# Three seven-product pairs in the second up stage of a residual block, in place of two

## The chip, the cores and the metric

The kernel runs on one core of one Trainium2 chip. The metric is the device time of one execution in microseconds (us), the median of three runs. TensorE (PE in the profile) multiplies matrices; VectorE (DVE), ScalarE (ACT) and GpSimd (POOL) do the element-wise work; SyncE (SP) issues most of the DMAs and POOL some.

## What is computed

One layer of a residual network on 512 tokens of width 1024 in float32. Only its last part, the channel mixer, is touched by the change:

```
h = rms_norm(x, norm_ffn_g)
up = causal_dwconv(h @ w_up, conv_ffn_w)        # 1024 -> 2 x 2816, three taps
a, b = split(up)
x = x + (silu(a) * b) @ w_down                  # 2816 -> 1024
return rms_norm(x, norm_f_g)
```

`causal_dwconv` weighs each token's value with those of the two tokens before it, column by column.

## The kernel before

**Products.** Everything is held transposed, with the model's columns on the 128 partitions and the 512 tokens along the free axis. A float32 weight is split into a high and a low part (`wh` by ScalarE, L275; `wl` by VectorE, L279), and so are the inputs. A product is the sum of three passes, high by high, low by high and high by low, each a matmul of a 128x128 weight block with 256 tokens.

**Pairs and phases.** The hidden width is 22 blocks of 128. Block `j` of `a` and block `j` of `b` make the up pair `j`. The pairs 0 to 11 are phase 0 and 12 to 21 phase 1 (`PHASES`); after each phase's up stage comes its down stage, in which the finished hidden blocks are multiplied by `w_down`.

**Plain and seven-product pairs.** A plain pair (`block`, `mm3`, L309) is two weight chunks of eight 128x128 blocks (`up2j`, `up2j+1`), each 48 matmuls. A pair listed in `SUP` is done by `seven` instead, a Winograd scheme: of each two-by-two arrangement of weight blocks with the two halves of the tokens, seven products are formed in place of eight (`PROD`, `passes`, L327). Such a pair is two doubles; each double is a chunk `P` of six weight blocks (18 matmuls) and a chunk `F` of eight blocks of weight sums (24 matmuls). The down stages use the same scheme throughout (`STEPS`: 12 doubles in phase 0, 8 in phase 1). A plain pair leaves two PSUM banks, which are multiplied by the norm factor (`mul`, L1171) and run through the three taps (`tap`: one ScalarE and two VectorE instructions, L566, L567, L570). A seven-product pair leaves four banks, which `merge` first adds up (L1192 to L1206) and scales (L1214). `glu` then takes silu of `a` (L1231) and multiplies by `b` on POOL (`ge` for an even pair, L1236; `go` for an odd one, L1243); after an odd pair it forms sums for the down stage (`t13`, `t24`, L1253 to L1258) and splits them (`hl`, L1262 and L1263). For the very last pair, `glu` also calls a Sqrt activation (L1233) for the sake of its table.

**Inputs of the seven-product up pairs.** They need sums of the inputs too (`up_forms`). Phase 0 makes them and stores them in DRAM (`ys`); for phase 1 four tiles `y` are loaded back through one buffer, one after the other (L1084), and split (`parts_of`, L1076 and L1079). That work comes due at the end of the down stage of phase 0 and in the first two weight chunks of phase 1.

**Weight sums.** The `F` chunks are made in DRAM while the kernel runs (`make_forms`): for each group of two doubles six DMAs, `put f0` (512 KB, SP, L208), `add f0` (512 KB, POOL, accumulating, L211), `put f1`, `add f1`, `put f2`, `add f2` (256 KB each), each waiting for the one before it. `GROUPS` says at which call of `slot()` each of the six is issued, and how far the next group is shifted. `slot()` is called twice in every up pair and once in every double of a down stage. In phase 0 the count runs from 8 to 31 in the up stage and from 32 to 43 in the down stage.

**Weights and buffers.** The chunks come in a fixed order (`stream`), loaded by SP up to seven ahead into four buffers for plain and `P` chunks and four for `F` chunks. `split` makes `wh` and `wl` of one chunk, while PE works on the chunk before it; there are two buffers for `wh` and two for `wl`, so a split can start only when PE has finished the chunk two before.

**The order of the small work.** VectorE and ScalarE have more to do between the splits than fits at once, so tasks wait in a list `later`, each with a planned cost and a due chunk. After each split `run_later` releases tasks up to a budget. While a task of an up pair's evacuation (tag `e`) waits, the budget is 4.2 us after a plain chunk, 1.6 after a `P` and 1.2 after an `F` (L290); without one it is 1.7, 1.6 and 0.75. The planned costs are 6.87 us for the merge and the taps of a seven-product pair, 4.2 for the evacuation of a plain pair, and 4.5 for the sums and splits of each two pairs. If no `e` task waits, an evacuation is issued at once. `after_split` makes released tasks follow the latest split on their engine. The framework may otherwise issue an instruction of ScalarE or VectorE ahead of one that was written earlier; matmuls, POOL's products of pairs before the last and DMAs keep the written order.

**The end of an up stage.** At the second chunk of the last pair (L1162 on) the first `P` chunk of the down stage is split. Then, if `e` tasks still wait, they are all issued (`flush_only`) and the first `F` chunk is split (`split()`). If none waits, neither is done there; that `F` chunk is split later, by `seven`, behind the last evacuation and `glu`.

**Banks.** The seven-product pairs of phase 1 use PSUM banks 2 to 5, the plain pairs banks 6, 7, 0, 1 in turn (`turns`).

Of the kernel before, what the change touches and what calls it, by code (L numbers as in the profile page):

```python
# [16 lines left out]
KB = D // P  # L17
# [25 lines left out]
PHASES = ((0, 12), (12, NP))  # L43
# [14 lines left out]
PLAIN = [(m, k) for m in (6, 7) for k in range(*PHASES[1])]  # L58
PCUTS = (0, 8, 12, 20)

SUP = ((1, 2, 5), (14, 16))
XF = (26, 0)
UPD = tuple(tuple(((j, q), (j, q + 1)) for j in js for q in (0, 2)) for js in SUP)
DOUBLES = GATES + UPD[0] + STEPS[0] + UPD[1] + STEPS[1]
NU = [len(GATES), len(GATES + UPD[0] + STEPS[0])]
ND = [NU[i] + len(UPD[i]) for i in range(2)]
GROUPS = {"gate": (2, 4, 1), "up0": (2, 4, 1), "up1": (2, 4, 1), 0: (2, (0, 3, 14, 18, 22, 26), 1), 1: (2, 3, 1)}


@with_exitstack  # L70
def block_kernel(ctx, tc, xT, vecs, wv, win, wmix, wo, wup, wst, wdp, outT):
# [10 lines left out]
    def keep(ins):  # L82
        return tc.keep_in_program_order(ins)
# [45 lines left out]
    def step_chunks(n):  # L129
        m = len(DOUBLES[n])  # L130
        return [(f"P{n}", wst[n, :, : 3 * m * P], 3 * m * P), (f"F{n}", n, 4 * m * P)]
# [10 lines left out]
    for ph, (j0, j1) in enumerate(PHASES):  # L142
        for j in range(j0, j1):
            if j in SUP[ph]:
                stream += step_chunks(n) + step_chunks(n + 1)
# [13 lines left out]
    def after_split():  # L159

        st = ExitStack()
        for ins in order.values():
            st.enter_context(tc.issue_after(ins))
        return st
# [25 lines left out]
    def make_forms(n0, n1, key, start=0):  # L190

        size, step, shift = GROUPS[key]
        if not start:
            make_forms.slot = 0
        cuts = [n0]
        for n in range(n0 + 1, n1 + 1):
            if n == n1 or n - cuts[-1] == size or len(DOUBLES[n]) != len(DOUBLES[cuts[-1]]):
                cuts.append(n)
        for g, (a, b) in enumerate(zip(cuts, cuts[1:])):
            m = len(DOUBLES[a]) * P  # L200
            f = dr.tile([P, b - a, 4 * m], F32, tag=f"f{a}", name=f"f{a}")
            w = wst[a:b].rearrange("n p c -> p n c")
            x0, x1, x2 = w[:, :, 3 * m : 5 * m], w[:, :, 5 * m : 7 * m], w[:, :, 7 * m : 8 * m]
            for n in range(a, b):
                made[n] = f[:, n - a, :]

            def put(dst, src):
                return lambda: keep(nc.sync.dma_start(dst, src))  # L208

            def add(dst, src):  # L210
                return lambda: keep(nc.gpsimd.dma_start(dst, src, accum_op=ALU.add))  # L211

            f0, f1, f2 = f[:, :, : 2 * m], f[:, :, 2 * m : 3 * m], f[:, :, 3 * m :]
            ops = (put(f0, x0), add(f0, x1), put(f1, f[:, :, :m]), add(f1, x1[:, :, m:]), put(f2, f1), add(f2, x2))
            todo_bg.extend((start + (step * k if isinstance(step, int) else step[k]) + shift * g, op) for k, op in enumerate(ops))
        todo_bg.sort(key=lambda w: w[0])
# [30 lines left out]
    def flush_only(tags):  # L247

        while n := [n for n, w in enumerate(later) if set(w[2]) & set(tags)]:
            with after_split():  # L250
                later.pop(n[0])[3]()
# [495 lines left out]
    acc, bank_s, bank_t = ring(2, 0, 1), ring(3, 4), ring(5, 6)  # L747
# [116 lines left out]
    acc = ring(3, 4, 5, 6, 2, 7)  # L864
# [94 lines left out]
    for j in range(KB):  # L959
# [13 lines left out]
        else:  # L973
            if j == GJ:
                acc = ring(3, 4, 2, 7)
# [31 lines left out]
    acc = ring(0, 1, 5, 6, 3, 4, 2, 7)  # L1007
# [89 lines left out]

    po = None
    make_forms(ND[0], ND[0] + len(STEPS[0]), 0)
    make_forms(NU[1], ND[1], "up1", 20)  # L1100
    for j in range(KB):
        slot()
        if j == 0:
# [20 lines left out]
    def turns(*ids):  # L1124
        st = list(ids)

        def f(name):
            f.last = st.pop(0)
            flush((f.last,))
            return bank(f.last, name)  # L1130

        return f

    acc = turns(0, 1, *(2, 3, 4, 5) * 2, 6, 7, 0, 1, 2, 3, 4, 5)
    USETS = dict.fromkeys(SUP[1], (2, 3, 4, 5)) | {1: (2, 3, 4, 5), 2: (6, 7, 0, 1), 5: (6, 7, 0, 1)}
    ssq3 = xp.tile([P, S], F32, tag="ssq", name="ssq3")
# [4 lines left out]
    def up(j, ph, rb2, pu=None):  # L1141
        uu = []

        def tap(i, z):
            u = fp.tile([P, S], F32, tag="fu", name=f"fu{j}{i}", bufs=3)
            taps(u, z, CF + 3 * (2 * j + i))
            uu.append(u)

        if j in SUP[ph]:
            c = 2 * SUP[ph].index(j)  # L1150
            slot()
            seven(
                UPD[ph][c : c + 2], NU[ph] + c, {j: USETS[j]}, lambda q, g: up_form(ph, q, g), of="x",
                done=lambda i, banks, ids: merge(ph, j, banks, ids, rb2, tap, uu),
            )
            slot()
            return
        evacs = []
        for i in range(2):
            slot()  # L1160
            p = pu[i] if pu else block(f"up{2 * j + i}", x1h, x1l, True)
            if i and j + 1 == PHASES[ph][1]:  # L1162
                split_next()
                if any(("e",) in w[2] for w in later):
                    flush_only((("e",),))
                    split()
            z = [None]

            def mul(i=i, p=p, z=z):
                z[0] = fp.tile([P, S], F32, tag="fz", name=f"fz{j}{i}", bufs=4)  # L1170
                nc.vector.tensor_mul(z[0], p, rb2)  # L1171

            evac = [(0.7, mul), (1.4, lambda i=i, z=z: tap(i, z[0]))]
            if i:
                evac.append((0, lambda: glu(ph, j, uu)))
            if any(("e",) in w[2] for w in later):
                later.extend((0, us, (("e",), acc.last) if x == 0 else (("e",),), f) for x, (us, f) in enumerate(evac))
            else:
                for _, f in evac:
                    f()  # L1180
# [141 lines left out]
    X, Y = (6, 7, 0, 1), (2, 3, 4, 5)  # L1322
    for ph, (j0, j1) in enumerate(PHASES):
        if ph:
            acc = turns(*(6, 7, 0, 1) * 4)
            make_forms(ND[1], len(DOUBLES), ph)
        for j in range(j0, j1):
            pu = None
            if j == 0:
                nrm = {}  # L1330

                def mid():
                    nrm["c"] = rstd_col([ssq2], NT, 6, "n2")

                def late():
                    nrm["b"] = rstd_sb(rstd_bc(nrm["c"], NT, 7, "n2"), "n2")

                pu = lead(["up0", "up1"], x1h, x1l, mid, late)
            up(j, ph, nrm["b"], pu)
        if not ph:  # L1340
            up_forms(0, 1)
        flush_only((("e",),))
        seven(
            STEPS[ph], ND[ph], ({0: X, 1: Y, 3: X, 2: Y}, {0: X, 1: Y, 2: Y})[ph],
            lambda q, g: (gh[:, place(ph, q) + g, :], gl[:, place(ph, q) + g, :]),
            done=lambda i, banks, ids: combine(ph, i, banks, ids), tick=True,
        )
        assert not todo_bg
# [188 lines left out]
```

## Time and profile before

| what | us |
|---|---|
| median of three runs | 695.37 (695.27 to 695.41) |
| the profiled execution | 694.18 |
| its span, first to last instruction | 692.4 |
| up stage of phase 1 on PE, first matmul to the first of the down stage | 523.83 to 631.08 |
| PE busy over the span | 683.1 (99%) |
| VectorE busy over the span | 554.2 (80%) |
| ScalarE busy over the span | 368.3 (53%) |

A row of the timeline has the start and the duration in us, the engine, the line of the kernel, the operation, the output and inputs by the program's names, the shapes, the number of instructions merged into the row and, in brackets, how long the engine had been idle before it and what ended that. `dn` is the PSUM output of `seven`, `p_up` that of a plain pair. A matmul's row lasts longer than the step from one matmul to the next, since they are pipelined; so PE's pace is read from the starts. A row of the windows has, for one stretch, its length and the busy time of each engine with the number of instructions, then the granted TensorE clock (1.00 is full), the mean busy share of the 16 DMA engines and GB/s.

### The profile page before, as it was taken

What the parts mean: (1) busy time and instruction counts of PE and PEld (TensorE: products, weight loads), DVE (VectorE), ACT (ScalarE), POOL (GpSimd) and SP (SyncE); (2) the same over time, 40 slices, a digit from 0 to 9 for tenths busy, and PEclk for the clock granted to TensorE, in tenths of its full rate; (3) what the DMA queues carried; (4) which work ended last, traced back from release to release, by engine and by line L of the source; (5) the groups of instructions that cost most, each with busy time, mean ns of one, the idle gap of its engine ahead of it and who ended that gap; (6) DMA issues with size and microseconds to landing.
All of it is one profiled execution on the core that took longest, in us unless ns stands there. A gap on an engine that the chain in (4) does not pass through costs nothing. (4 is left out here: it accounts for less than half of the span.)

```text
span 692.4 us, 14690 instructions
## 1 busy us (share of the span) xinstructions
PE 683.1 (99%) x5936; PEld 680.6 (98%) x5936; DVE 554.2 (80%) x858; ACT 368.3 (53%) x579; POOL 190.5 (28%) x201
## 2 busy tenths in 40 slices
PE   9999999999999999999999999999999999999996
PEld 9999999999999999999999999999999999999995
DVE  6677787877578778769879699998787899988894
ACT  5675755554554444546554555545444544545572
POOL 6134947542020201214400144340100325231000
PEclk9999999999999999999999999999999999999998
DMA  8629999552568586788998498888945996676413
GB/s 308 225 67 293 216 243 204 134 120 92 185 144 221 166 268 205 230 308 213 158 313 241 126 233 222 200 242 231 252 149 167 337 231 157 188 168 182 154 31 122
DMA packets 65012, 137.53 MB, mean 199 GB/s; under 512 B 5760, under 2 KB 30352, under 8 KB 64688
## 3 DMA queue, kind: packets, MB, share of 16 engines
q1 hardware_dynamic: 44664, 107.28, 47.2%
q0 software_dynamic: 18464, 26.03, 23.4%
q10 hardware_dynamic: 1816, 3.29, 1.3%
q8 instruction: 46, 0.75, 0.4%
q14 instruction: 22, 0.18, 0.1%
HBM read 132.31 MB, written 47.71 MB: 260 GB/s over the span
## 5 line engine op out<-in xcount | busy, mean ns | idle before, releaser
L211 POOL DMA_DIRECT2D f<-in_wst_dram x66 | 77.7, 1371 | 27.1 <-DMA f<-f 26.8
L309 PE MATMUL p_up<-x1h,wh_up 128*128 128x256 f32 x416 | 81.2, 276 | 0.0
L309 PE MATMUL p_up<-x1l,wh_up 128*128 128x256 f32 x416 | 81.0, 276 | 0.0
L309 PE MATMUL p_up<-x1h,wl_up 128*128 128x256 f32 x416 | 81.0, 276 | 0.0
L279 DVE TENSOR_TENSOR wl_F<-raw_F,wh_F 128x1024 fp32r<-128x1024 f32 (+1 forms) x42 | 55.9, 1330 | 20.0 <-ACT wh_F L275 20.0
L275 ACT ACTIVATE wh_F<-raw_F 128x1024 fp32r<-128x1024 f32 (+1 forms) x42 | 44.3, 1054 | 39.5 <-PE dn L327 28.7
L309 PEld LDWEIGHTS p_up<-x1h,wh_up 128*128 128x128 f32 x416 | 62.7, 188 | 0.0
L309 PEld LDWEIGHTS p_up<-x1l,wh_up 128*128 128x128 f32 x416 | 62.7, 188 | 0.0
L309 PEld LDWEIGHTS p_up<-x1h,wl_up 128*128 128x128 f32 x416 | 62.6, 188 | 0.0
L309 PE MATMUL p_in<-xgh,wh_in 128*128 128x256 f32 x288 | 56.8, 279 | 0.0
L309 PE MATMUL p_in<-xgh,wl_in 128*128 128x256 f32 x288 | 56.6, 278 | 0.0
L309 PE MATMUL p_in<-xgl,wh_in 128*128 128x256 f32 x288 | 56.5, 278 | 0.0
L279 DVE TENSOR_TENSOR wl_P<-raw_P,wh_P 128x768 fp32r<-128x768 f32 (+1 forms) x42 | 41.7, 992 | 14.7 <-ACT wh_P L275 8.6
L327 PE MATMUL dn<-gh,wh_F 128*128 128x256 f32 x216 | 51.2, 277 | 1.2 <-ACT wh_F L275 1.2
L275 ACT ACTIVATE wh_P<-raw_P 128x768 fp32r<-128x768 f32 (+1 forms) x42 | 35.1, 835 | 32.1 <-PE dn L327 23.2
L327 PE MATMUL dn<-gl,wh_F 128*128 128x256 f32 x216 | 51.0, 276 | 0.0
L1236 POOL TENSOR_TENSOR ge<-fu,fu 128x512 f32<-128x512 f32 x11 | 20.1, 1831 | 110.5 <-DVE fu L570 85.6
L279 DVE TENSOR_TENSOR wl_up<-raw_up,wh_up 128x1024 fp32r<-128x1024 f32 x34 | 43.8, 1288 | 7.4 <-ACT wh_up L275 7.4
L275 ACT ACTIVATE wh_up<-raw_up 128x1024 fp32r<-128x1024 f32 x34 | 35.8, 1054 | 19.4 <-PE p_up L309 9.3
L309 PEld LDWEIGHTS p_in<-xgh,wh_in 128*128 128x128 f32 x288 | 44.7, 188 | 0.7
L309 PEld LDWEIGHTS p_in<-xgl,wh_in 128*128 128x128 f32 x288 | 43.7, 188 | 0.0
L309 PEld LDWEIGHTS p_in<-xgh,wl_in 128*128 128x128 f32 x288 | 43.6, 188 | 0.0
(343 smaller groups left out, 2211.8 us busy)
## 6 DMA issues: line engine op xcount, KB each, us to landing
raw_F<-f SPq DMA_DIRECT2D x41, 512.0 KB, 5.7
raw_up<-in_wup_dram SPq DMA_DIRECT2D x34, 512.0 KB, 5.6
raw_P<-in_wst_dram SPq DMA_DIRECT2D x41, 384.0 KB, 5.4
raw_in<-in_win_dram SPq DMA_DIRECT2D x24, 512.0 KB, 3.6
f<-in_wst_dram POOLq DMA_DIRECT2D x41, 256.0 KB, 6.8
f<-in_wst_dram SPq DMA_DIRECT2D x20, 512.0 KB, 7.1
f<-in_wst_dram POOLq DMA_DIRECT2D x20, 512.0 KB, 9.1
f<-f SPq DMA_DIRECT2D x40, 256.0 KB, 6.5
```

Of the source, the lines that this page charges most:

```text
L211: return lambda: keep(nc.gpsimd.dma_start(dst, src, accum_op=ALU.add))
L275: ins = nc.scalar.activation(hi, raw, AF.Copy)
L279: ins = nc.vector.tensor_sub(lo, raw, hi.bitcast(F32))
L309: keep(nc.tensor.matmul(out[:, cs], w, x[:, cs], start=start and i == 0 and c == 0, stop=stop and i == 2 and c == len(cut) - 1,))
L327: keep(nc.tensor.matmul(out, wl if x == 1 else wh, xl if x == 2 else xh, start=opens and bk not in seen, stop=closes and bk not in left,))
L1236: keep(nc.gpsimd.tensor_mul(ge, a.rearrange(halves_of, h=2), b.rearrange(halves_of, h=2)))
```

## The change

Phase 1 does the pairs 13, 15 and 17 in seven-product steps instead of 14 and 16. So its order becomes 12 plain, 13 seven, 14 plain, 15 seven, 16 plain, 17 seven, then 18 to 21 plain. The list of banks for the plain pairs is cut from 16 to 14 entries.

There are three groups of weight sums for them in place of two. Their 18 DMAs are issued at slots 30 to 40 (each group at 0, 2, 3, 5, 6 and 8 from its start, the groups one slot apart) in place of 12 at slots 20 to 41 (every four slots): almost all in the down stage of phase 0, where before they lay mostly in its up stage.

At the end of an up stage, if `e` tasks still wait, the first `F` chunk of the down stage is now split before they are issued.

```diff
-SUP = ((1, 2, 5), (14, 16))
+SUP = ((1, 2, 5), (13, 15, 17))
...
-GROUPS = {"gate": (2, 4, 1), "up0": (2, 4, 1), "up1": (2, 4, 1), 0: (2, (0, 3, 14, 18, 22, 26), 1), 1: (2, 3, 1)}
+GROUPS = {"gate": (2, 4, 1), "up0": (2, 4, 1), "up1": (2, (0, 2, 3, 5, 6, 8), 1), 0: (2, (0, 3, 14, 18, 22, 26), 1), 1: (2, 3, 1)}
...
-    make_forms(NU[1], ND[1], "up1", 20)
+    make_forms(NU[1], ND[1], "up1", KB + 2 * PHASES[0][1] - 2)
...
             if i and j + 1 == PHASES[ph][1]:
                 split_next()
                 if any(("e",) in w[2] for w in later):
+                    split()
                     flush_only((("e",),))
-                    split()
...
         if ph:
-            acc = turns(*(6, 7, 0, 1) * 4)
+            acc = turns(*(6, 7, 0, 1) * 3, 6, 7)
             make_forms(ND[1], len(DOUBLES), ph)
```

## The prediction

> **What bounds the kernel now.** I read the page's busy times first, then PE's timeline for idle time, then the rows of VectorE, ScalarE and SP around each stop.
>
> ```profile
> span 692.4 us, 14690 instructions
> PE 683.1 (99%) x5936; PEld 680.6 (98%) x5936; DVE 554.2 (80%) x858; ACT 368.3 (53%) x579; POOL 190.5 (28%) x201
> ```
>
> PE is the bound. A change can win only by taking matmuls away or by closing PE's few stops, and it loses by opening new ones. PE's timeline, at the starts of chunks and at each stop from 468 on:
>
> ```profile
> 468.62 0.38 PE L327 MATMUL dn<-gh,wh_F 128*128 128x256 f32 x1 [0.66 <-ACT wh_F L275]
> ...
> 523.83 0.28 PE L327 MATMUL p_up<-x1h,wh_up 128*128 128x256 f32 x1
> ...
> 545.59 0.28 PE L327 MATMUL dn<-x1h,wh_P 128*128 128x256 f32 x1
> ...
> 554.72 0.38 PE L327 MATMUL dn<-x1h,wl_F 128*128 128x256 f32 x1 [0.35 <-DVE wl_F L279]
> 555.76 0.28 PE L327 MATMUL p_up<-x1h,wh_up 128*128 128x256 f32 x1
> ...
> 566.64 0.28 PE L327 MATMUL dn<-x1h,wh_P 128*128 128x256 f32 x1
> ...
> 576.16 0.28 PE L327 MATMUL p_up<-x1h,wh_up 128*128 128x256 f32 x1
> ...
> 610.02 0.73 PE L327 MATMUL p_up<-x1h,wl_up 128*128 128x256 f32 x4 [0.15 <-DVE wl_up L279]
> ...
> 631.08 0.28 PE L327 MATMUL dn<-gh,wh_P 128*128 128x256 f32 x1
> ...
> 633.78 0.38 PE L327 MATMUL dn<-gh,wh_F 128*128 128x256 f32 x1 [0.50 <-ACT wh_F L275]
> ```
>
> Plain pair 15 lasts 566.64 - 555.76 = 10.88 us for 96 matmuls; seven-product pair 16 lasts 576.16 - 566.64 = 9.52 for 84. Both give 0.1133 us a matmul, so a `P` (18) takes 2.04 and an `F` (24) 2.72. Pair 14 took 10.17, so its stop at 554.72 cost 0.65. The first `P` of the last down stage began at 631.08 and should have ended at 633.12; its `F` began at 633.78: 0.66 lost. (The bracket is smaller because the modelled end of a matmul lies behind its slot.)
>
> **The saved matmuls.** One pair more in seven products: 12 matmuls, 10.88 - 9.52 = **-1.36 us**. That is 0.20% of 695.37, and 0.2% (1.39 us) is about what a measurement of this kernel can tell from no change. So every stop counts.
>
> **The middle of the stage.** A seven-product pair brings more splitting and merging to VectorE, and by the planner's costs more tasks wait than before: 14.87 us at the first chunk after the last such pair, against 8.27. I still charge nothing there, because phase 0 does the same with its pairs 1, 2 and 5 while a list of that length waits. A window after them:
>
> ```profile
> 400.00:430.00 30.00, 30.00 (x267) 30.00 (x266) 29.47 (x44) 15.51 (x23) 14.93 (x12) 1.00 0.92 228
> ```
>
> VectorE is busy 29.47 of 30 us, PE without a stop. The stop at 610 I leave as it is. The stop at 554.72 I take out, **-0.65**: its cause is VectorE waiting, ahead of the weights, for POOL's product of pair 13 just before pair 14:
>
> ```profile
> 551.82 0.43 DVE L1254 TENSOR_TENSOR go<-go,ge 128x256 f32<-128x256 f32 x1 [1.19 <-POOL go L1243]
> ```
>
> Now pair 13's product is issued during pair 14 and its sums come due in pair 15, two chunks later at the least. If it only moves, the term is 0.
>
> **The start of pair 13.** It now begins where the plain pair 13 began, one plain pair behind the down stage: 523.83 + 10.88 = 534.71. Its third product writes bank 3 (`PROD`, the set 2 to 5), four matmuls in, at 535.16. Bank 3 still holds a sum of the down stage's last pair, read by L1294. Plain pair 13 used banks 0 and 1 and had no such wait. The rows of ScalarE and of VectorE at that place:
>
> ```profile
> 533.00 1.06 ACT L1076 ACTIVATE gh<-y 128x1024 fp32r<-128x1024 f32 x1 [1.73 <-DMA y<-ys]
> 536.08 0.63 ACT L1231 ACTIVATE fu<-fu 128x512 f32<-128x512 f32 x1 [2.01 <-DVE fu L570]
> 536.62 1.05 ACT L275 ACTIVATE wh_up<-raw_up 128x1024 fp32r<-128x1024 f32 x1
> ```
>
> ```profile
> 534.10 1.23 DVE L1079 TENSOR_TENSOR gl<-y,gh 128x1024 fp32r<-128x1024 f32 x1 [1.46 <-ACT gh L1076]
> 535.24 0.74 DVE L570 SCALAR_TENSOR_TENSOR fu<-fz,vec,fu 128x510 f32<-128x510 f32 x1
> 535.90 0.68 DVE L1294 TENSOR_TENSOR xm<-xm,dn 128x512 f32<-128x512 f32 x1
> ```
>
> VectorE stands still for the last input tile `y`, then does a tap, then L1294, which ends at 536.58. So PE waits from 535.16 to 536.58: **+1.4**. Everything behind the waiting matmul on PE moves with it. The split of pair 13's first `F` stands where `wh_up` stands at 536.62, behind the silu, and ends at 537.67. Without the bank's wait it would be 0.92 late (the `P` would end at 536.75); with it the `P` ends at 538.2 and the split is hidden. Bounds: 0, if L1294 is issued before the tile's split, since its input is ready at 524; and the tile's lateness one for one above 1.4. I take 1.4, since these instructions come in this order today.
>
> **The end of the up stage.** Call T the end of the last up chunk on PE. Counting the planner's costs chunk by chunk, in the kernel before nothing waits there, so the branch with the swapped lines isn't entered (nor in phase 0, before or after: the stop at 468.62 stays). In the changed kernel 5.90 us wait when the first `P` is split; one task of these, the taps of chunk `up42`, has the tag `e`. The branch is entered, and the first `F` is split ahead of the silu and the Sqrt of the last pair. Before, it stood behind them:
>
> ```profile
> 630.54 0.63 ACT L1231 ACTIVATE fu<-fu 128x512 f32<-128x512 f32 x1 [2.15 <-DVE fu L570]
> 631.19 1.28 ACT L1233 ACT_TABLE_LOAD   x1
> 632.49 0.29 ACT L1233 ACTIVATE tbl<-fu,ex 32x1 f32<-32x1 f32 x1
> 632.69 1.04 ACT L275 ACTIVATE wh_F<-raw_F 128x1024 fp32r<-128x1024 f32 x1
> ```
>
> The buffer came free at about 631.1, and 1.5 us passed. Now `wh_F` starts at T and is done a microsecond before the `F` is due: **-0.66**.
>
> But what stood ahead of that split now stands behind it: the taps of `up42`, the taps of `up43`, silu and table, and the four splits of pairs 18 and 19, which the second double needs. Before, by the same count, those splits were issued with the last two up chunks. What they take on VectorE:
>
> ```profile
> 633.76 1.23 DVE L279 TENSOR_TENSOR wl_F<-raw_F,wh_F 128x1024 fp32r<-128x1024 f32 x1 [1.79 <-ACT wh_F L275]
> 634.90 0.75 DVE L567 SCALAR_TENSOR_TENSOR fu<-fz,vec,fu 128x511 f32<-128x511 f32 x1
> 635.57 0.95 DVE L279 TENSOR_TENSOR wl_P<-raw_P,wh_P 128x768 fp32r<-128x768 f32 x1
> 636.44 0.74 DVE L570 SCALAR_TENSOR_TENSOR fu<-fz,vec,fu 128x510 f32<-128x510 f32 x1
> ...
> 644.70 1.89 DVE L1263 TENSOR_TENSOR gl<-go,gh 128x512 fp32r<-128x512 f32 x3
> ```
>
> By the starts, `wl_F` takes 1.14, a tap 0.67 + 0.66, `wl_P` 0.87; a split of pairs 0.63. From T: 1.04 until `wh_F` is there, then 1.14 + 0.63 + 2 x 1.33 + 3 x 0.63 + 0.87 = 7.19, so `wl` of the second `P` is there at T + 8.23. It is due at 2.04 + 2.72 + 12 x 0.1133 = T + 6.12: 2.1 late. At 636.44 the second half of a tap stood behind `wl_P`; if it does so again, 8.23 - 0.66 = 7.57, 1.45 late. **+1.45**. Bounds: 0, with both taps behind the weights; 2.6, with ScalarE in its worst order (a rival, below).
>
> **DMAs.** The 18 transfers of weight sums move to the down stage of phase 0. SP will stand at puts that wait for POOL's adds, and raw weights queue behind. From the page's list of issues, and the cover of the raw weights:
>
> ```profile
> raw_F<-f SPq DMA_DIRECT2D x41, 512.0 KB, 5.7
> ...
> f<-in_wst_dram POOLq DMA_DIRECT2D x20, 512.0 KB, 9.1
> ```
>
> ```profile
> 469.86 0.32 SPq L182 DMA_DIRECT2D raw_F<-f  x1
> ```
>
> ```profile
> 485.04 1.07 ACT L275 ACTIVATE wh_F<-raw_F 128x1024 fp32r<-128x1024 f32 x1 [1.65 <-PE dn L327]
> ```
>
> This is the fifth `F` of that stage: issued at 469.86, it is wanted at 485.04 and takes 5.7 to land, 9.5 us of slack. An add lands 9.1 us after its issue and the next put comes one double (4.76) later, so I count waits of 4 to 6 us at single puts: charged nothing, hidden by that slack. What DMA contention could do is a rival below.
>
> **The sum.** -1.36 - 0.65 + 1.4 - 0.66 + 1.45 = +0.18. The profiled execution took 694.18 (the span and 1.8 around it), so it would take 694.4; the median of the runs shown lies 1.19 higher, and on it the forecast is 695.37 + 0.18 = **695.55**. Its own range is 694.0 to 696.75, the band within 0.2%.
>
> **Rivals.**
>
> *The savings stand.* L1294 and the second `P` are issued early enough, and neither new stop appears: -1.36 - 0.65 - 0.66 = -2.67, **692.7**; with a remnant of one, up to 693.9. For it: both inputs are ready in time, and only the order of issue decides. Against: today's rows have the unhelpful order in both places. Chance 0.21.
>
> *The input tiles come late* (slower). The transfers' cost, by queue, and the DMA share in the two stretches:
>
> ```profile
> q1 hardware_dynamic: 44664, 107.28, 47.2%
> q0 software_dynamic: 18464, 26.03, 23.4%
> ```
>
> ```profile
> 466.00:510.00 44.00, 43.34 (x383) 43.15 (x381) 34.87 (x49) 22.02 (x29) 2.05 (x2) 1.00 0.82 224
> 510.00:535.00 25.00, 25.00 (x223) 25.00 (x222) 19.04 (x25) 12.20 (x14) 0.00 (x0) 1.00 0.47 150
> ```
>
> That is 3.05 us of all 16 engines for a MB on q1 and 6.2 on q0. A group (1.05 MB put, 1.05 MB added) costs 9.7; three, less two early puts, 25.9 in that stage, where 8.1 are now: 17.8 more. Until 510 only 0.18 x 44 = 7.9 is free, so 10 spill into the time when the `y` tiles are fetched one after the other:
>
> ```profile
> 517.09 5.97 SPq L1084 DMA_DIRECT2D y<-ys  x2
> ```
>
> ```profile
> 520.38 1.06 ACT L1076 ACTIVATE gh<-y 128x1024 fp32r<-128x1024 f32 x1 [0.95 <-DMA y<-ys]
> ```
>
> ```profile
> 522.61 1.22 DVE L279 TENSOR_TENSOR wl_up<-raw_up,wh_up 128x1024 fp32r<-128x1024 f32 x1
> ```
>
> The second tile took 3.3 us. The splits of the first up chunk stand behind it; the low one ends at 523.83 and is wanted eight matmuls after 523.83, at 524.73. It decides from 0.9 us on. At 2 us later PE loses 1.1 there and the rest, about 0.9, at pair 13: **697.6**. Against: the spill may be over by 520. Chance 0.27.
>
> *ScalarE decides at T.* `wh_F` 1.0, one split 0.6, two taps' copies 1.3, three splits 1.7, silu 0.6, table 1.3, the Sqrt 0.2 and `wh_P` 0.8 make 7.5 before the second `P`, due at 4.76: 2.7 in place of 1.45, **696.8**. Chance 0.07. [...]
>
> *The branch isn't entered* (no `e` task is left): the 0.66 stays, the late splits come earlier, about half of the 1.45 goes: **695.5**. Chance 0.05. The forecast keeps 0.40.
>
> **Chances and range.** Faster: 0.21. Within 0.2%: 0.40 + 0.05 + half of ScalarE's = 0.49. Slower: 0.27 + 0.03 = 0.30. The range reaches down into the first rival and up past 697.6: 693.0 to 698.2.
>
> **What would show it.** Pair 13's first `P` with a gap after four matmuls, released by VectorE L1294; no stop at the last stage's first `F`, but one in or before its second `P`; pairs 15 and 17 of 9.52 us. Wrong would be a stop at the first up chunk of phase 1 (the tiles), at a down chunk of phase 0 (raw weights), or late weights inside pairs 15 and 17.

## The result, and the profile after

The changed kernel takes 699.72 us (median of 7 runs, 697.83 to 701.12) against 695.37 before: ratio 1.0064, 95% interval 1.0054 to 1.0075, so it is **slower** by 0.6%, outside the predicted range. The medians differ by 4.35. Its profiled execution took 698.97, 4.79 more than the profiled one of before. The page's head after:

```profile
span 697.2 us, 14695 instructions
...
PE 682.9 (98%) x5924; PEld 679.9 (98%) x5924; DVE 560.5 (80%) x865; ACT 370.0 (53%) x582; POOL 190.1 (27%) x204
```

There are 12 matmuls less, and a span 4.8 us longer: PE waits. Its timeline after, at starts of chunks and at each stop:

```profile
525.22 0.39 PE L327 MATMUL p_up<-x1h,wh_up 128*128 128x256 f32 x1 [1.28 <-ACT wh_up L275]
526.67 0.73 PE L327 MATMUL p_up<-x1h,wl_up 128*128 128x256 f32 x4 [0.26 <-DVE wl_up L279]
...
538.74 0.39 PE L327 MATMUL dn<-gh,wh_P 128*128 128x256 f32 x1 [1.28 <-DVE xm L1294]
...
558.80 0.28 PE L327 MATMUL dn<-x1h,wh_P 128*128 128x256 f32 x1
...
568.32 0.28 PE L327 MATMUL p_up<-x1h,wh_up 128*128 128x256 f32 x1
...
632.24 0.28 PE L327 MATMUL dn<-gh,wh_P 128*128 128x256 f32 x1
...
634.28 0.28 PE L327 MATMUL dn<-gh,wh_F 128*128 128x256 f32 x1
...
637.60 0.38 PE L327 MATMUL dn<-gh,wh_P 128*128 128x256 f32 x1 [0.44 <-ACT wh_P L275]
...
640.74 0.97 PE L327 MATMUL dn<-gh,wl_P 128*128 128x256 f32 x6 [1.09 <-DVE wl_P L279]
...
651.96 0.38 PE L327 MATMUL dn<-gl,wh_P 128*128 128x256 f32 x1 [1.36 <-DVE gl L1263]
```

I measure a stop as the step between two starts less 0.1133; in the table the slower steps right beside it are counted with it, which adds some 0.1. Pair 15 lasts 568.32 - 558.80 = 9.52 us, and nothing stops inside it. The first `F` of the last down stage now follows its `P` after 634.28 - 632.24 = 2.04. At 637.60 and 640.74 one chunk stops twice, for its high and for its low part. The four places with a stop are new:

| place | us against before |
|---|---|
| 12 matmuls less | -1.36 |
| stops at 554, 610 and the first `F` gone (0.65, 0.5, 0.7) | -1.85 |
| first up chunk of phase 1 (525.22, 526.67) | +2.2 |
| pair 13's first `P` (538.74) | +1.56 |
| second `P` of the last down stage (637.60 to 640.74) | +2.5 |
| fourth `P` there (651.96) | +1.77 |
| sum (measured: +4.79) | +4.8 |

**First up chunk.** The second input tile is issued by SP, and VectorE and ScalarE hold the first up chunk's split behind it. Rows of SP, ScalarE and VectorE, after:

```profile
517.03 0.33 SPq L1084 DMA_DIRECT2D y<-ys  x1
```

```profile
523.16 1.06 ACT L1076 ACTIVATE gh<-y 128x1024 fp32r<-128x1024 f32 x1 [3.79 <-DMA y<-ys]
524.13 1.99 ACT L275 ACTIVATE wh_up<-raw_up 128x1024 fp32r<-128x1024 f32 x2
```

```profile
525.39 2.35 DVE L279 TENSOR_TENSOR wl_up<-raw_up,wh_up 128x1024 fp32r<-128x1024 f32 x2
```

The tile was issued at the same time as before (517.09) and taken up (ScalarE's split of it, L1076) 6.1 us later in place of 3.3. The DMA engines at that time, in the windows of before and then of after (the last three columns are the granted clock, DMA share and GB/s):

```profile
512.00:518.00 6.00, 6.00 (x55) 6.00 (x55) 5.59 (x8) 2.86 (x3) 0.00 (x0) 1.00 0.27 87
```

```profile
466.00:510.00 44.00, 43.34 (x382) 43.14 (x382) 34.69 (x50) 22.01 (x29) 6.17 (x6) 1.00 1.02 269
...
512.00:518.00 6.00, 6.00 (x56) 6.00 (x55) 5.59 (x8) 2.87 (x3) 0.00 (x0) 1.00 1.11 329
```

The down stage of phase 0 is full (1.02), and what doesn't fit there is still running at 512 to 518: a share of 1.11 in place of 0.27. It is over soon after: from 520 to 525 the share is 0.10 (before 0.27).

**Pair 13.** VectorE's rows after:

```profile
536.20 1.22 DVE L1079 TENSOR_TENSOR gl<-y,gh 128x1024 fp32r<-128x1024 f32 x1 [1.58 <-ACT gh L1076]
537.34 0.74 DVE L570 SCALAR_TENSOR_TENSOR fu<-fz,vec,fu 128x510 f32<-128x510 f32 x1
538.00 0.68 DVE L1294 TENSOR_TENSOR xm<-xm,dn 128x512 f32<-128x512 f32 x1
```

The order is the one of before: idle until the last tile, its split, a tap, then L1294, which frees bank 3 at 538.68.

**The second `P`.** ScalarE and VectorE after, from T = 632.24:

```profile
632.44 1.06 ACT L275 ACTIVATE wh_F<-raw_F 128x1024 fp32r<-128x1024 f32 x1 [3.56 <-PE p_up L309]
633.41 0.62 ACT L1262 ACTIVATE gh<-ge 128x512 fp32r<-128x512 f32 x1
633.93 1.32 ACT L566 ACTIVATE fu<-fz,vec 128x512 f32<-128x512 f32 x2
635.16 1.66 ACT L1262 ACTIVATE gh<-go 128x512 fp32r<-128x512 f32 x3
636.72 0.83 ACT L275 ACTIVATE wh_P<-raw_P 128x768 fp32r<-128x768 f32 x1
```

```profile
635.28 1.41 DVE L567 SCALAR_TENSOR_TENSOR fu<-fz,vec,fu 128x511 f32<-128x511 f32 x2
636.61 1.40 DVE L570 SCALAR_TENSOR_TENSOR fu<-fz,vec,fu 128x510 f32<-128x510 f32 x2
637.93 1.89 DVE L1263 TENSOR_TENSOR gl<-go,gh 128x512 fp32r<-128x512 f32 x3
639.74 0.95 DVE L279 TENSOR_TENSOR wl_P<-raw_P,wh_P 128x768 fp32r<-128x768 f32 x1
```

`wh_F` stands at T as forecast. Ahead of the second `P`'s weights ScalarE does two taps' copies and four splits behind it. VectorE does four halves of taps and four splits (the first, of `ge`, at 634.68, isn't shown). The high part is 0.6 late, the low part the rest.

**The fourth `P`** waits for the last split of the last pair's sums:

```profile
650.08 1.22 DVE L279 TENSOR_TENSOR wl_F<-raw_F,wh_F 128x1024 fp32r<-128x1024 f32 x1
651.22 0.69 DVE L1263 TENSOR_TENSOR gl<-go,gh 128x512 fp32r<-128x512 f32 x1
```

In the code, `glu` counts the due chunks of these tasks from `k = len(parts) - 1`, the splits done so far. The branch has just split one chunk more (the first `F`), so each of the tasks comes due one chunk later than before.

### The profile page after: what moved, and what is told of

Its sections match the earlier page's. It is cut to its first block, busy times and chain, and to the rows that moved or that the text cites. A ratio compares the mean times of both kernels' runs of the same rounds, so it can differ in the third digit from the quotient of the medians.

```text
span 697.2 us, 14695 instructions
## 1 busy us (share of the span) xinstructions
PE 682.9 (98%) x5924; PEld 679.9 (98%) x5924; DVE 560.5 (80%) x865; ACT 370.0 (53%) x582; POOL 190.1 (27%) x204
## 5 line engine op out<-in xcount | busy, mean ns | idle before, releaser
L309 PE MATMUL p_up<-x1h,wh_up 128*128 128x256 f32 x392 | 76.4, 276 | 0.0
L309 PE MATMUL p_up<-x1h,wl_up 128*128 128x256 f32 x392 | 76.3, 276 | 0.0
L309 PE MATMUL p_up<-x1l,wh_up 128*128 128x256 f32 x392 | 76.3, 276 | 0.0
L279 DVE TENSOR_TENSOR wl_F<-raw_F,wh_F 128x1024 fp32r<-128x1024 f32 (+1 forms) x44 | 58.3, 1325 | 20.4 <-ACT wh_F L275 20.3
L309 PEld LDWEIGHTS p_up<-x1h,wl_up 128*128 128x128 f32 x392 | 59.0, 188 | 0.0
L309 PEld LDWEIGHTS p_up<-x1h,wh_up 128*128 128x128 f32 x392 | 59.0, 188 | 0.0
L309 PEld LDWEIGHTS p_up<-x1l,wh_up 128*128 128x128 f32 x392 | 59.0, 188 | 0.0
L327 PE MATMUL dn<-gh,wh_F 128*128 128x256 f32 x228 | 54.0, 277 | 0.7 <-ACT wh_F L275 0.7
L327 PE MATMUL dn<-gl,wh_F 128*128 128x256 f32 x228 | 53.9, 276 | 0.0
L327 PEld LDWEIGHTS dn<-gh,wh_F 128*128 128x128 f32 x228 | 42.8, 188 | 0.9 <-ACT wh_F L275 0.9
```

What stands on the lines that cost most here:

```text
L279: ins = nc.vector.tensor_sub(lo, raw, hi.bitcast(F32))
L309: keep(nc.tensor.matmul(out[:, cs], w, x[:, cs], start=start and i == 0 and c == 0, stop=stop and i == 2 and c == len(cut) - 1,))
L327: keep(nc.tensor.matmul(out, wl if x == 1 else wh, xl if x == 2 else xh, start=opens and bk not in seen, stop=closes and bk not in left,))
```

## The experiments

All ratios are to the kernel before on the same chip, with 95% intervals.

| kernel | pairs in seven products | other edits | ratio |
|---|---|---|---|
| `e1_early_sums` | 13, 15, 17 | sums' DMAs as before | 1.0030 (1.0019 to 1.0040) |
| `e2_old_order` | 13, 15, 17 | evacuations ahead of `F`'s split | 1.0102 (1.0073 to 1.0131) |
| `e3_two_pairs` | 13, 15 | | 0.9985 (0.9975 to 0.9994) |
| `e4_banks` | 13, 15, 17 | pair 13 on banks 0, 1, 4, 5 | 1.0046 (1.0030 to 1.0062) |
| `b1_due` | 13, 15, 17 | due chunk | 1.0025 (1.0008 to 1.0042) |
| `b2_late_sums_alone` | 14, 16 | only the late sums | 0.9997 (0.9986 to 1.0007) |
| `c1_budget` | 13, 15, 17 | early sums, budget 4.9 | 0.9994 (0.9985 to 1.0004) |
| `c2_15_17_19` | 15, 17, 19 | as `c1_budget` | 0.9996 (0.9985 to 1.0007) |
| `f1_all_mends` | 15, 17, 19 | as `c2`, `F` first always, due chunk | 0.9993 (0.9984 to 1.0002) |
| `f2_15_17` | 15, 17 | early sums, `F` first always, due chunk | 0.9997 (0.9988 to 1.0007) |
| `f3_late_three` | 15, 17, 19 | `f1_all_mends` with the late sums | 1.0003 (0.9988 to 1.0018) |
| `f4_first_alone` | 14, 16 | `F` first always, due chunk | 1.0002 (0.9992 to 1.0011) |
| `h1_two_tiles_budget` | 13, 15, 17 | `c1_budget`, tiles in two buffers | 0.9988 (0.9972 to 1.0004) |
| `h2_two_tiles` | 13, 15, 17 | due chunk, tiles in two buffers | 1.0015 (1.0006 to 1.0024) |
| `h3_two_pairs_two_tiles` | 13, 15 | tiles in two buffers | 0.9980 (0.9971 to 0.9990) |
| `h4_first_held` | 14, 16 | `f4_first_alone`, evacuation held | 0.9993 (0.9983 to 1.0003) |
| `k1_two_pairs_held` | 13, 15 | `h3` with `F` first, evacuation held | **0.9969** (0.9960 to 0.9978) |
| `k2_three_pairs_held` | 13, 15, 17 | all mends | 0.9990 (0.9981 to 0.9999) |

### The sums' transfers: e1, b2, f3

```diff
-"up1": (2, (0, 2, 3, 5, 6, 8), 1)
+"up1": (2, 4, 1)
...
-    make_forms(NU[1], ND[1], "up1", KB + 2 * PHASES[0][1] - 2)
+    make_forms(NU[1], ND[1], "up1", 20)
```

`e1_early_sums` makes this edit to the kernel after, `b2_late_sums_alone` the reverse to the kernel before (two groups), and `f3_late_three` is `f1_all_mends` (below) without it.

> The changed kernel with its three groups of weight sums issued as before (slots 20 on, every four slots; 42 at the last). Theory: the first up chunk of phase 1 starts late (2.2 us of lost slots at 525.22 and 526.67 in the changed kernel) because the sums' DMAs spill into the fetch of the second input tile. Then that stop goes to under 0.4 us and the median falls by about 2, to 697.5 to 698; the three other stops (pair 13's first P 1.55, second P of the last down stage 2.5, fourth P 1.77) stay. Rival: the tile is late because pair 13's own raw P and F chunks (0.9 MB) are fetched just ahead of it, at 513; then the stop stays above 1.5 us and the median stays at 699 to 700.

> The kernel before with the late and denser weight sums of the change for its two groups, nothing else. Theory one (the transfers in the down stage delay the input tiles of phase 1, so the first up chunk's low weights come late): a stop of 0.5 to 2 us eight matmuls after the start of the up stage, 695.6 to 697.4; two groups in place of three may make it shorter. Rival (the stop belongs to the order of VectorE's work with pair 13 first in line; the transfers alone do nothing): no stop at the first up chunk, 695.4 within 0.3, as three pairs less one with the late sums showed no such stop.

> As the first kernel of this set, but with the change's late and dense weight sums for its three groups. It tells whether the stop of up to 2.2 us at the first up chunk of phase 1 belongs to the transfers of three groups or to pair 13. Theory one (three groups spill past the down stage, two don't): the second input tile lands late, the first up chunk's low weights come 0.5 to 2.2 us late, the time is 0.6 to 2.3 above the kernel with early sums and spreads more from run to run. Rival (pair 13's place in the order makes it): no stop there, the same time within 0.3.

With the early sums the first up chunk has no stop; the window of `e1_early_sums`:

```profile
512.00:518.00 6.00, 6.00 (x55) 6.00 (x54) 5.59 (x8) 2.87 (x3) 0.00 (x0) 1.00 0.48 156
```

By the ratios, 2.4 of the 4.4 us went. The late sums of two groups alone leave a share of 0.31, no stop there and the same time. Three late groups give 1.08 to 1.11 in each kernel that has them, whatever its pairs. But the stop doesn't come each time: the profiled executions of `f3_late_three` and `e4_banks` had none. It follows the second tile. From issue to take-up the tile took 3.4 us in `e1_early_sums`, 3.6 in `f3_late_three` and 4.0 in `e4_banks`, with no stop; 5.3 in `e2_old_order` with 1.3 us lost, 5.6 in `b1_due` with 1.7, 6.1 in the kernel after with 2.2. So in these executions PE lost one for one what the tile took above 3.9. The runs of `f3_late_three` went from 694.42 to 698.45, and those of `f1_all_mends` with early sums from 694.59 to 695.16. So it is the third group that spills, and how late the tile gets differs from execution to execution. That the long runs of `f3_late_three` had the stop at this place is inferred; none of them was profiled.

### What the list holds at the end: e2, b1, c1

```diff
                 if any(("e",) in w[2] for w in later):
-                    split()
                     flush_only((("e",),))
+                    split()
```

```diff
         q, k = j // 2, len(parts) - 1
+        if j + 1 == PHASES[ph][1]:
+            k = chunk.n
```

```diff
-            run_later(k, {"u": 4.2, "P": 1.6, "F": 1.2}[nm[0]])
+            run_later(k, {"u": 4.9 if nm[0] == "u" and int(nm[2:]) > 23 else 4.2, "P": 1.6, "F": 1.2}[nm[0]])
```

The first is `e2_old_order`, the second `b1_due`, the third, with early sums, `c1_budget`.

> The changed kernel with the old order at the end of an up stage: the waiting evacuations first, then the first F chunk. Theory: the work of VectorE and ScalarE behind the last up chunk is the same and only its place changes, so the F is late by 0.5 to 0.9 again, the second P by that much less, and the time stays within 0.5 us of the changed kernel's; the fourth P stays late by 1.8 in both. Rival: the swap is what opens the 2.5 us at the second P, and undoing it gives back 1 us or more.

> Only the due chunk of the last pair's sums is counted from the chunk in work, not from the splits done. Theory one (the branch splits one chunk more, so all tasks of the last pair come due one chunk late and are found missing by the fourth P of the last down stage): the stop of 1.77 us before that P goes, and the time falls by 1.5 to 1.9 us against the kernel after, that is to 697.2 to 698.2 on the scale on which it takes 699.7. Rival (VectorE has simply too much to do between 635 and 652, whatever is due when): the stop moves to the third or second P or stays, the time falls by less than 0.5 us, and weights split between 640 and 650 come late instead.

> The kernel after with the weight sums issued early again (as before) and a budget of 4.9 us in place of 4.2 after the plain chunks of phase 1. By the planned costs the list then has no evacuation left at the last pair, the branch isn't entered and the last pair's tasks keep their due chunks. Theory one (both stops of the last down stage, 2.5 and 1.77 us, come from what is left in the list when the up stage ends): both go, the stop of about 0.7 at the first F comes back, pair 13's wait of 1.2 to 1.6 stays: against the kernel with early sums alone, 1.9 + 0.6 + 1.7 - 0.7 = 3.5 less, 693.3. Rival (VectorE has no room for 4.9 us beside a weight split in 5.44 us of PE): late weights in pairs 14, 16 and 18 to 21, 0.3 to 0.5 us in each of six or more chunks, 695 to 697.

`e2_old_order`: the second `P` is nearly in time (0.17 in place of 2.5), but the first `F` comes 3.1 us late, and then its matmuls run at 0.213 us, half the pace (below). Neither expectation had that. With a list this long the new order is the better one: from 631 on, the profiled execution loses 6.9 us here and 4.3 in the kernel after. By the ratios it is so too (1.0102 against 1.0064), though their intervals overlap a little.

`b1_due`: the stop at the fourth `P` is gone. Starts of the fourth and the fifth `P` chunk on PE:

```profile
652.15 0.28 PE L327 MATMUL dn<-gh,wh_P 128*128 128x256 f32 x1
656.91 0.28 PE L327 MATMUL dn<-gh,wh_P 128*128 128x256 f32 x1
```

They follow at 4.76, a `P` and an `F` without a stop. VectorE had room for the same work: only its due chunk was wrong. By the ratios 2.7 us went, more than the 1.77; but the runs of `b1_due` go from 695.88 to 700.55, so it is the trace and not the ratio that shows this stop gone.

`c1_budget`: no `e` task is left at the end (the branch isn't entered: `wh_F` stands behind silu and table load again), and both stops of the last down stage are gone, nor does one come back at the first `F`; so the second `P`'s lateness is what was left over. A part came back where the budget was raised, 0.63 at pair 15 and 1.2 at 611, where weights came late. So the rival has its share: by the ratios 2.5 us were gained against `e1_early_sums`, in place of 3.5.

### Pair 13's wait: e4, e3, h1, h2, h3

```diff
-    USETS = dict.fromkeys(SUP[1], (2, 3, 4, 5)) | {1: (2, 3, 4, 5), 2: (6, 7, 0, 1), 5: (6, 7, 0, 1)}
+    USETS = dict.fromkeys(SUP[1], (2, 3, 4, 5)) | {13: (0, 1, 4, 5), 1: (2, 3, 4, 5), 2: (6, 7, 0, 1), 5: (6, 7, 0, 1)}
```

```diff
-        y = (gx if ph or q % 2 else hp).tile([P, 4, 2 * P], F32, tag="y", name=f"y{ph}{q}")
+        if ph and q % 2:
+            y = fp.tile([P, 6, 2 * P], F32, tag="gr", name=f"y{ph}{q}")[:, :4, :]
+        else:
+            y = (gx if ph or q % 2 else hp).tile([P, 4, 2 * P], F32, tag="y", name=f"y{ph}{q}")
...
-            if ph and q < 3:
-                up_forms(q + 1, ph)
+            if ph and q < 2:
+                up_forms(q + 2, ph)
...
             up_forms(0, 1)
+            at = [c[0] for c in stream].index(f"F{ND[0] + len(STEPS[0]) - 4}")
+            later.append((at, 0, (("x", 1),), lambda: up_forms(1, 1)))
```

The first is `e4_banks` (with the list of banks to match). The second fetches the second and fourth tile into another buffer, beside the first and third: in `h1_two_tiles_budget`, `h2_two_tiles`, `h3_two_pairs_two_tiles`. `e3_two_pairs` drops pair 17.

> The changed kernel with pair 13 in PSUM banks 0, 1, 4, 5, whose readers of the down stage are done early, and the plain pairs 14 to 21 in banks 6, 7, 0, 1, 6, 7 and so on. Theory: pair 13's first P no longer waits for VectorE L1294 (1.55 us lost); its first F is then late by 0.9 behind the silu, as worked out in the prediction, so 0.6 to 1.5 us are won: 698.2 to 699.1. Rival: it is the late input tile and not the bank that the P waits for; then nothing is won.

> The changed kernel with pairs 13 and 15 alone in seven products (17 is plain, two groups of weight sums, still late). Theory: by the planner's costs the list of waiting tasks runs empty before the last pair, so the branch isn't entered, and the stops at the second and the fourth P (2.5 and 1.77) go, the stop of 0.7 to 0.8 at the first F comes back, 1.36 us of matmuls come back; pair 13's stop of 1.55 stays; the start stop shrinks to about 1 with a third fewer DMAs. Sum against the changed kernel: -4.3 + 0.75 + 1.36 - 1.2, 3 to 3.5 us faster, about 696.5. Rival: the stops at the end come from ScalarE's table load and silu whatever the list holds; then a stop of over 1.5 us stays behind the first double.

> The budget kernel (pairs 13, 15, 17, early sums, 4.9) with the second and the fourth input tile of phase 1 in another buffer, so that they are fetched beside the first and the third and not behind them. Theory one (pair 13's wait is VectorE standing still for the last tile with L1294 behind it): VectorE gets to L1294 some 3 us sooner and the wait of 1.4 us goes: 695.3 - 1.4 = 693.9. Rival (VectorE has that much work before L1294 in any case): the wait stays within 0.4 us, 695.2.

> The kernel after, with its late and dense sums, the due chunk counted from the chunk in work, and the input tiles in two buffers. Theory one (both the stop of 2.2 us at the first up chunk and pair 13's wait of 1.4 to 2.8 come from the serial fetch of the tiles among the sums' transfers): both go, and the long runs with them: 697.3 - 1.5 - 0.5 to 1.5 = 694.5 to 695.5 with a spread below 1.5 us (4.7 us without). What is left is the second P of the last down stage (2.5). Rival (the transfers delay the raw weights and the tiles whatever the buffers): the stops and the spread of some 4 us stay, 696 to 697.5.

> The kernel with the pairs 13 and 15 and the change's late sums, with the input tiles in two buffers. Theory one: its one stop of about 1 us in pair 13 goes, 0.9 less than with one buffer, ratio to before 0.9985 - 0.0013 = 0.997. Rival (VectorE busy in any case): the same as with one buffer, ratio 0.9985.

With other banks the first `P` runs through, and then its `F` is 1.93 late, because the split of that `F` also stands behind the last tile. Two pairs with late sums keep the wait (0.95) and lose every other new stop. The wait, too, follows a tile, the fourth. It is taken up 2.2 us ahead of pair 13's start in `e3_two_pairs` and 1.07 us are lost; 1.7 ahead in the kernel after, with 1.56; 1.4 ahead in `e2_old_order`, with 1.95; 0.45 ahead in `b1_due`, with 2.85. With two buffers the wait is gone from all three kernels; VectorE in `c1_budget`, then in `h1_two_tiles_budget`:

```profile
536.12 0.68 DVE L1294 TENSOR_TENSOR xm<-xm,dn 128x512 f32<-128x512 f32 x1
```

```profile
531.63 0.74 DVE L567 SCALAR_TENSOR_TENSOR fu<-fz,vec,fu 128x511 f32<-128x511 f32 x1
532.29 0.68 DVE L1297 TENSOR_TENSOR xm<-xm,dn 128x512 f32<-128x512 f32 x1
```

L1297 is what was L1294; with no tile to wait for it starts 3.8 us sooner, before the bank is wanted. So the cause was the fetch, and the bank only the way by which it reached PE. The ratio of `h1_two_tiles_budget` has a wide interval because of two long runs (695.9 and 697.75); its median is 1.45 us below that of before, against 0.3 in `c1_budget`. In `h2_two_tiles` the stop at the first up chunk stayed (1.0 and 0.4): the third tile, issued at 517.8, was taken up 5.7 us later, at 523.5, with a DMA share of 1.09 from 512 to 518. For that stop the rival holds: the transfers delayed a tile with two buffers as well.

### The first F in front, alone: f4, h4

```diff
-                if any(("e",) in w[2] for w in later):
-                    flush_only((("e",),))
+                if ph:
                     split()
+                    flush_only((("e",),))
...
                 for _, f in evac:
-                    f()
+                    if i and j + 1 == NP:
+                        with after_split():
+                            f()
+                    else:
+                        f()
```

`f4_first_alone` has the first hunk on the kernel before, `h4_first_held` both; both have the due chunk of `b1_due`.

> The kernel before with one part of the change alone, in force without the condition on what is left in the list: the first F of the last down stage is split ahead of the last evacuation (due chunk counted from the chunk in work). Theory one (before, the list is empty there, so nothing is displaced): the stop of 0.66 at that F goes, 0.66 less than before, ratio 0.9990. Rival (the taps, silu and table load make the second P late even so): 0 to 1 us late at the second P, no gain or slower by up to 0.3.

> The kernel before with the first F of the last down stage split in front, and the last pair's evacuation, silu and table load held behind that split (in the other kernel of this kind the framework issued them ahead of it). Theory one (as the prediction had it): the stop of 0.66 at the first F goes, and with nothing else in the list the second P isn't late: 0.5 to 0.7 less than before, ratio 0.9991. Rival (the held work makes the second P late by as much): no stop at the first F, 0.4 to 1 us at the second P, ratio 1.000.

`f4_first_alone` didn't test it: written first, the split was still issued last. ScalarE there, then in `h4_first_held`:

```profile
631.57 0.63 ACT L1233 ACTIVATE fu<-fu 128x512 f32<-128x512 f32 x1 [2.16 <-DVE fu L570]
632.22 1.28 ACT L1235 ACT_TABLE_LOAD   x1
...
633.72 1.04 ACT L275 ACTIVATE wh_F<-raw_F 128x1024 fp32r<-128x1024 f32 x1
```

```profile
631.94 1.07 ACT L275 ACTIVATE wh_F<-raw_F 128x1024 fp32r<-128x1024 f32 x1 [2.91 <-PE p_up L309]
632.90 0.61 ACT L1237 ACTIVATE fu<-fu 128x512 f32<-128x512 f32 x1
633.42 0.83 ACT L275 ACTIVATE wh_P<-raw_P 128x768 fp32r<-128x768 f32 x1
634.27 1.28 ACT L1239 ACT_TABLE_LOAD   x1
```

Held behind the split, the silu and the table load cost nothing: no stop at the first `F`, none at the second `P`. The ratio, 0.9993, is what the 0.66 asks for (0.9991), though its interval also holds 1.

### What three pairs are worth: c2, f1, f2, k1, k2

`c2_15_17_19` is `c1_budget` with `(15, 17, 19)`; `f1_all_mends` and `f2_15_17` have the first hunk above and not the second. `k1_two_pairs_held` is `h3_two_pairs_two_tiles` with both hunks and the due chunk; `k2_three_pairs_held` has three pairs, early sums, two buffers, both hunks, the due chunk, and a budget of 4.9 behind pair 17 alone (`> 35`).

> As the budget kernel, with the seven-product pairs 15, 17 and 19 in place of 13, 15 and 17. Theory one (bank 3 and the late input tile cost only because the first such pair follows the down stage by one plain pair; a pair that starts behind an even plain pair has no other stop): pair 13's wait of 1.2 goes, no stop before pair 15, 4.5 us left in the list at the end, no branch: 695.4 - 1.36 - 0.65 - 0.5 = 692.9, or 692.1 by the budget kernel's time less 1.2. Rival (pair 19 leaves too little time before the end, VectorE is late at the second P or at the fourth): 1 to 2 us back there, 694 to 695.

> The kernel with pairs 15, 17 and 19, early sums and the budget of 4.9, and besides the first F of the last down stage always split ahead of the last evacuation, with the due chunk counted from the chunk in work. Theory one (the 2.04 us that PE waited at that F were only the silu, the table load and the last taps in front of its split): the stop goes and nothing takes its place, 695.2 - 2.0 = 693.1. Rival (as in the kernel after, the work displaced makes the second P late): 0.5 to 1.9 us back there, 693.6 to 695.

> Two pairs, 15 and 17, with early sums and the old budget of 4.2, the first F always split first. No matmul is saved. Theory one (a pair behind an even plain pair has no stop in front, and the list is empty of evacuations at the end): before's stops of 0.65 at 554, 0.5 at 610 and 0.66 at the first F go, 695.5 - 1.8 = 693.7. Rival (the saved matmuls are what the better kernels gained by; order alone gives little): 695 to 695.6.

> Two pairs, 13 and 15, two buffers for the input tiles, the first F split first with the last evacuation held behind it. Theory one: the one stop left (0.5 at that F) goes, nothing is late at the second P since the list is empty: 693.6 - 0.5 = 693.1, ratio to before 0.997. Rival: 0.5 late at the second P, ratio 0.998.

> Three pairs, 13, 15 and 17, early sums, two buffers for the input tiles, a budget of 4.9 only for the chunks behind pair 17, the first F split first with the last evacuation held, and the due chunk counted from the chunk in work. Theory one (the saved matmuls stand once the stops are out): all four stops of before are gone and 12 matmuls less: before - 1.36 - 0.65 - 0.52 - 0.66 = 3.2 less, plus 0.2 to 0.5 at the second P by the planned costs (2.8 us left in the list), ratio 0.9960. Rival (VectorE is full behind pair 17: what was one late stop comes back in another place): 1 to 2.5 us of late weights between 590 and 640, ratio 0.9975 to 0.9990, no better than two pairs.

`c2_15_17_19` has no stop ahead of pair 15, but one of 0.6 at the first `F` of pair 17 and one of 2.0 at the first `F` of the last down stage. In `f1_all_mends` the first stayed and the second became 0.5 and 0.9 at the second `P`. `f2_15_17` stopped 1.25 at the first `F`, with the table in front as in `f4_first_alone`, and 0.5 at the second `P`. The gains that the first theories of these three asked for (1.8 to 3.3 us) didn't come. `k2_three_pairs_held` has no stop at the first up chunk, in pair 13 or at the fourth `P`; PE's stops that it has, the rows of VectorE and of ScalarE ahead of them, and the windows of before and then of `k2_three_pairs_held` behind pair 17's place (the third busy time is VectorE's):

```profile
620.15 0.75 PE L327 MATMUL p_up<-x1h,wl_up 128*128 128x256 f32 x4 [1.33 <-DVE wl_up L279]
636.49 0.39 PE L327 MATMUL dn<-gh,wh_P 128*128 128x256 f32 x1 [1.30 <-ACT wh_P L275]
```

```profile
618.08 2.02 DVE L279 TENSOR_TENSOR wl_up<-raw_up,wh_up 128x1024 fp32r<-128x1024 f32 x1
```

```profile
633.50 1.28 ACT L1242 ACT_TABLE_LOAD   x1
...
635.61 0.83 ACT L275 ACTIVATE wh_P<-raw_P 128x768 fp32r<-128x768 f32 x1
```

```profile
589.00:631.00 42.00, 41.85 (x369) 41.65 (x368) 37.15 (x53) 21.12 (x32) 13.47 (x10) 1.00 0.70 183
```

```profile
589.00:632.00 43.00, 41.67 (x368) 41.47 (x367) 41.39 (x59) 21.15 (x30) 11.41 (x10) 1.00 0.66 163
```

VectorE is busy 41.39 of 43 us there (96%; before 37.15 of 42, 88%), and two stops of 1.5 us each take back twice the 1.36. The first is VectorE's: taps and splits of sums stand ahead of the weights' split, and this split itself took 2.02 us where those at 604.84, 611.27 and 623.25 took 1.22 each; why it took longer isn't shown by a run. The second stop is ScalarE's: between `wh_F` (630.51) and `wh_P` it does the silu, the table load and the small Sqrt with it, a tap's copy and two splits, and is idle for only 0.23 us. That is the mechanism of the prediction's ScalarE rival. So a full VectorE accounts for one of the two stops, and whether another order on ScalarE would take out the other wasn't tried. With two pairs and the same mends PE ran from 475 to 655 without one stop, as this window of `k1_two_pairs_held` has it:

```profile
575.00:625.00 50.00, 50.00 (x444) 50.00 (x443) 45.28 (x65) 25.20 (x36) 15.11 (x13) 1.00 0.76 187
```

That version is the fastest, 692.67 against 695.29, ratio 0.9969 (0.9960 to 0.9978), without a matmul saved: it has only the stops taken out. (The profiled execution was its longest, 695.12; what made it long lies earlier, since its first `F` of phase 0's down stage already starts 2.65 us later than before.) The pairs 15, 17 and 19 were tried only without the last evacuation held, and other places for three not at all.

## Why the prediction was wrong

- **Saved matmuls, -1.36:** right.
- **The middle:** right to charge nothing in the kernel after; the stop at 554 went as said, and the one at 610, left in the sum, went too (-0.5).
- **Pair 13, +1.4:** right in place, instruction and size (1.56), with the wait growing one for one as the tile got later: 1.07 to 2.85 us among the executions.
- **First `F`, -0.66:** right, by `h4_first_held` as well.
- **Second `P`, +1.45:** the mechanism was right and the size was off: 2.5. Both second halves of the taps stood ahead of `wl_P` (the sum took one as behind), and ScalarE made `wh_P` 0.6 late. Silu and table load came behind `wh_P` (at 637.45 and 639.04), so of the ScalarE rival only the taps' copies and the splits happened; that its 2.7 lies near 2.5 is chance. The range ended at 698.2, 1.4 above ScalarE's 696.8; no run shows a term of 1.4 there: the table load's row lasts 1.28 us from 639.04, and the next row starts 0.02 after it.
- **Missing, +1.77:** the sum followed the branch up to the second `P` and never asked what else reads the number of splits. `b1_due` shows that `glu` does.
- **DMAs, charged nothing:** this step failed most. The raw weights were indeed covered (PE has no stop from 470 to 523); the input tiles weren't. It is the rival "the input tiles come late", and the sign that the prediction named for it: a spill past 510, the second tile later by 2.8 (2 were assumed), a stop of 2.2 in the up chunk. The point from which it decides was known, and the spill was worked out. What spoke against it, that the spill "may be over by 520", was so, but settles nothing: the tile is issued at 517 and was taken up at 520.4 before, so a spill that lasts to 520 lies over its whole fetch.

These misses make up the difference. In the profiled executions 4.79 was measured and 0.18 forecast; 2.2 + 1.05 + 1.77 + 0.16 (pair 13) - 0.5 (610) add up to 4.7, against the 4.6 between the two. The rival's 697.6 with the 1.05 and 1.77 added and the 0.5 taken off is 699.9, near the measured 699.72, but in part by luck: it put 1.1 into the up chunk and 0.9 at pair 13, where 2.2 and 0.16 were measured.

## What to carry to other kernels

When a change moves transfers, add up the DMA engines' time stage by stage, and look for the serial fetch that stands at the stage's end with work queued behind it; here a stage that overflowed by some microseconds hit that first. When a branch is newly taken, follow every variable that it moves (here the count of splits) to all who read it. When PE is 99% busy and another engine carries the small work, look at the stops before saving matmuls that cost the other engine time: here the stops alone gave 0.31% (`k1_two_pairs_held`), the stops and 12 matmuls less 0.10% (`k2_three_pairs_held`).

## What was not expected of the hardware

After a few of the stops TensorE ran at half pace for some 3.4 us: in `e2_old_order` after one of 3.1 us, in `b1_due` after 2.7, in `e4_banks` after 1.93; not after 2.04 in `c2_15_17_19`. Windows of `e2_old_order`, then of `c2_15_17_19` (the granted clock is the third column from the end):

```profile
634.00:636.00 2.00, 0.00 (x1) 0.00 (x0) 0.22 (x1) 1.97 (x4) 0.00 (x0) 1.00 0.00 0
636.00:638.00 2.00, 1.05 (x5) 1.05 (x6) 1.07 (x1) 2.00 (x4) 0.00 (x0) 0.74 0.00 0
638.00:640.00 2.00, 2.00 (x11) 2.00 (x11) 2.00 (x5) 2.00 (x5) 0.00 (x0) 0.50 0.40 88
640.00:642.00 2.00, 2.00 (x18) 2.00 (x18) 2.00 (x5) 1.39 (x2) 0.00 (x0) 0.91 0.44 174
```

```profile
632.00:634.00 2.00, 0.50 (x5) 0.30 (x3) 1.67 (x3) 2.00 (x4) 0.00 (x0) 1.00 0.82 331
634.00:636.00 2.00, 1.63 (x14) 1.63 (x15) 1.96 (x4) 1.06 (x2) 0.00 (x0) 1.00 0.12 48
```

At 0.213 in place of 0.1133 us a matmul, such a stretch (16 matmuls in `e4_banks`, 539.81 to 543.22) costs 1.6 us more than the stop itself. In these runs the length of a stop alone doesn't decide it: after one of 1.93 us the clock granted from 540 to 542 was 0.50 (`e4_banks`), after one of 2.04 it stayed at 1.00 (`c2_15_17_19`). What sets it off wasn't tried by itself.
